# One chunk of 64 tokens handled as a tile of 128 rows and columns, and token norms in overlapping tiles of 128

## The chip, the core and the metric

The kernel runs on one core of a Trainium2 chip. The metric is the device time of one execution in microseconds. Before the change it is 2760.29 us, the median of three runs (2759.63 to 2760.55). The engines are named as in the profile: PE multiplies matrices (PEld loads its stationary operand), DVE, ACT and POOL work elementwise, SP and POOL issue DMAs.

## What is computed

One layer is applied to 2048 prompt tokens and to 64 sample tokens, which have a state of their own. Its parts, cut to what matters:

```python
h = rms_norm(x, g_pre)
vA, bA, cA, zA, q, f, iv, zB, gA, gB = split_cols(h @ w_in)      # ten products of 1024 columns
yA = (silu(zA) * bA * causal_conv3(cA * vA)) @ w_a_out           # path A
fg = lb + (1 - lb) * sigmoid(f); logf = log(fg); k = 1 - fg      # path B, 8 heads of 128
for each chunk of 64 tokens:                                     # hgrn2_block, S is 128 x 128 a head
    b = cumsum(logf); ref = b at the middle of the chunk
    att = tril((q * exp(b - ref)) @ (k * exp(ref - b)).T)
    o = att @ v + (q * exp(b)) @ S
    S = exp(b_last) * S + (k * exp(b_last - b)).T @ v
yB = (o * rsqrt(mean(o * o)) * g_onorm * silu(zB)) @ w_b_out
out = (sigmoid(gA) * yA + sigmoid(gB) * yB) @ w_o
x = x + rms_norm(out, g_post)
x = x + (p @ w_ple_proj) * sigmoid(rms_norm(x, g_ple) @ w_ple_gate)
```

All of it is float32. The outputs are both token streams, the last two inputs of the convolution and the states S.

## The kernel before

The 2112 tokens lie in one row: 1344 of the prompt, the 64 of the sample, the other 704 of the prompt. They are taken in three blocks of 704, features on partitions and tokens on columns, so that a block is done in two halves of 352 columns (`HN`). Each large product is made of seven smaller ones (`sgroup`, `in_turn`: Strassen-like sums of weight blocks), and each float32 product is taken as three passes over a high and a low part (lines 343 to 345, 436 to 438, 469 to 471). One such pass is a matmul record of `128x352`. Weights are streamed from memory by SP.

A block runs path B (eight heads), then path A, then the merging products, the output product, the norms and the gate. Path B is the part that the change touches:

- `head_prep` makes the operands of a head in two `sgroup`s: queries `qe`, keys `kb` (for the second chunk of a pair already scaled), the keys `ka` of the first chunk of each pair packed side by side (line 761), values `vt`, `qx` for the product with the state, and the gate `z`.
- `head_attn` does the attention of a head for one part of a block. A block has 11 chunks of 64: ten go in pairs of 128 tokens, and the last is alone. So there are three parts (`plan`): part 0 with four pairs, part 1 with one pair, part 2 with the single chunk at columns 640 to 704 (in block 1 that chunk is the sample). Three blocks, eight heads and three parts make 72 runs of `head_attn`, 24 of each part.
- `head_attn` has four steps, each cut by a `yield`. Step 0 transposes keys and values (799, 801), copies them to SBUF on ACT (803, 804), and multiplies keys by queries (813, 815); DVE puts the result under a causal mask into the part's own buffer `att` (817, 819). Step 1 multiplies keys by values (825) and forms the states on DVE (842, 846). Step 2 multiplies by `att` (862) and by the state before (864) and takes the norm of each row (868 to 871, `rstd_of` on DVE and POOL). Step 3 transposes back (876) and applies the gate (878).
- `path_b` puts these steps into a list of hooks, first step 0 of the three parts, then step 1, and so on, with `keep_z` as the fourteenth and last. After each of the seven products of an `sgroup` one hook runs. So the attention of a head is spread over the two `sgroup`s of the next head, and `placed()` ties its matmuls on PE behind the product that has just been issued: on PE they always stand between two stretches of `128x352` records.

With the pairs every matmul of step 1 to 3 has 128 rows and 128 columns of stationary operand. With the single chunk they have 64 of one or both, and in part 1 the product with `ka` has 64 columns (line 812).

The token norms of a half (`rms`, `col_rstd`, `spread`) sum over features with a matmul by ones, which puts tokens on partitions: 352 tokens are tiles of 128, 128 and 96. `rstd_of` scales on DVE and raises to the power -0.5 on POOL, once for the full tiles and once for the 96. A matmul with the identity spreads the result again. `row_rstd` does the same from token rows for the next block.

Tiles come from pools. A tag has a number of buffers, and a tile waits until a buffer of its tag has been read for the last time. Those that matter here: `one` (8 buffers, the small tiles of parts 1 and 2), `s0` (2), `state` (`NH + 2` = 10).

Of the kernel before, what the change touches and what calls it, by code (L numbers as in the profile page):

```python
# [18 lines left out]
P = 128  # L19
# [63 lines left out]
def hybrid_step(  # L83
# [39 lines left out]
    def hf(n=HN):  # L123
        return ring.tile([P, HN], F32, tag="hf", name=nm("hf"), bufs=HALVES)[:, :n]
# [32 lines left out]

    def constants():
        tri = rt(P)
        G.memset(tri, 1.0)  # L160
        G.affine_select(
            out=tri, in_=tri, pattern=[[1, P]], compare_op=ALU.is_ge, fill=0.0, base=0, channel_multiplier=-1
        )
        V.tensor_copy(caus, tri)
        V.memset(keep, 1.0)
        V.memset(keep.rearrange("p (c t) -> p c t", t=CH)[:, :, 0:1], 0.0)
        for t in atts:
            V.memset(t, 0.0)
# [354 lines left out]
    def tiles_of(n):  # L523
        return [(i, i * P, min(P, n - i * P)) for i in range((n + P - 1) // P)]

    def rstd_of(ms_ap, out_ap, scale):
        V.tensor_scalar(out_ap, ms_ap, scale, EPS, ALU.mult, ALU.add)
        shape = [out_ap.shape[0], out_ap.shape[1]]
        G.tensor_tensor(out_ap, out_ap, mhalf[: shape[0], :].to_broadcast(shape), ALU.pow)
# [21 lines left out]
    def col_rstd(acc, n):  # L551

        pc = ps_attn()
        cols = cols_tile(n)
        with placed():
            for i, o, ln in tiles_of(n):
                T.matmul(pc[:ln, i : i + 1], acc[:, o : o + ln], ones, start=True, stop=True)
        nf = n // P
        if nf:
            rstd_of(pc[:, :nf], cols[:, :nf], 1.0 / D)  # L560
        if n % P:
            rstd_of(pc[: n % P, nf : nf + 1], cols[: n % P, nf : nf + 1], 1.0 / D)
        return cols
# [23 lines left out]
    def row_rstd(bl, out):  # L587

        out.extend(cols_tile(HN) for _ in bl["segs"])
        todo = [(cols, s["t0"] + o, i, ln) for cols, s in zip(out, bl["segs"]) for i, o, ln in tiles_of(HN)]  # L590
        nxt = []
        for n in range(0, len(todo) + 2, 2):
            now, nxt = nxt, []
            for cols, o, i, ln in todo[n : n + 2]:
                xts = [rt(512), rt(512)]
                for q, xt in enumerate(xts):
                    G.dma_start(xt[:ln], x_tok[o : o + ln, q * 512 : q * 512 + 512])
                nxt.append((cols, i, ln, xts))
            for cols, i, ln, xts in now:
                sc = small.tile([P, 2], F32, tag="ss2", name=nm("ss2"))  # L600
                for q, xt in enumerate(xts):
                    A.activation(xt[:ln], xt[:ln], AF.Square, accum_out=sc[:ln, q : q + 1])
                V.tensor_tensor(sc[:ln, 0:1], sc[:ln, 0:1], sc[:ln, 1:2], ALU.add)
                rstd_of(sc[:ln, 0:1], cols[:ln, i : i + 1], 1.0 / D)
# [115 lines left out]
    def head_prep(bl, hc, hd, first):  # L720
# [21 lines left out]
        ka, kb, qx, vt, z = hf(), rt(), rt(), rt(), rt()  # L742

        def scaled(after):
# [36 lines left out]
    def head_attn(ip, gs, d, hd):  # L781

        nt, ln = len(gs), gs[0]["len"]
        o0, n = gs[0]["off"], nt * ln
        qe, z, att = d["qe"], d["z"], atts[ip]

        def tile3():
            if nt == 1:
                return small.tile([P, 1, P], F32, tag="one", name=nm("one"), bufs=8)
            return cols3(rt(nt * P), nt)  # L790

        def keys(g):
            return d["kb"][:, g["off"] : g["off"] + ln]
# [3 lines left out]
        with placed():  # L797
            for i, g in enumerate(gs):
                T.transpose(p_k[:ln, i * P : i * P + P], keys(g), ident)
            for i, g in enumerate(gs):  # L800
                T.transpose(p_v[:ln, i * P : i * P + P], d["vt"][:, g["off"] : g["off"] + ln], ident)
        kt, v = tile3(), tile3()
        A.copy(kt[:ln], cols3(p_k, nt)[:ln])
        A.copy(v[:ln], cols3(p_v, nt)[:ln])
        p_a = ps_attn()
        with placed():
            for i, g in enumerate(gs):
                o = g["off"]
                if nt > 1:
                    own, rows = d["ka"][:, o // 2 : o // 2 + P], P  # L810
                else:
                    own, rows = d["ka"][:, o // 2 : o // 2 + CH] if ln == P else keys(g), CH
                T.matmul(p_a[:rows, i * P : i * P + CH], own, qe[:, o : o + CH], start=True, stop=True)
# [9 lines left out]
        with placed():  # L823
            for i in range(nt):
                T.matmul(p_u[:, i * P : i * P + P], kt[:ln, i, :], v[:ln, i, :], start=True, stop=True)  # L825
# [3 lines left out]
        if sample:  # L829
            cur = small.tile([P, P], F32, tag="s0", name=nm("s0"), bufs=2)  # L830
# [13 lines left out]
        if g["end"]:  # L844
            end = small.tile([P, P], F32, tag="state", name=nm("state"), bufs=NH + 2)
# [12 lines left out]
        with placed():  # L858
            for i, g in enumerate(gs):
                o = g["off"]  # L860
                dst = p_o[:ln, i * P : i * P + P]
                T.matmul(dst, att[:ln, i, :ln], v[:ln, i, :], start=True, stop=prevs[i] is None)  # L862
                if prevs[i] is not None:
                    T.matmul(dst, d["qx"][:, o : o + ln], prevs[i], start=False, stop=True)  # L864
        on = tile3()
        ms = small.tile([P, 4], F32, tag="ms", name=nm("ms"))
        po3 = cols3(p_o, nt)
        A.activation(on[:ln], po3[:ln], AF.Square)
        V.tensor_reduce(ms[:ln, :nt], on[:ln], axis=mybir.AxisListType.X, op=ALU.add)
        rstd_of(ms[:ln, :nt], ms[:ln, :nt], 1.0 / P)  # L870
        V.tensor_tensor(on[:ln], po3[:ln], ms[:ln, :nt].unsqueeze(2).to_broadcast([ln, nt, P]), ALU.mult)
        yield
        p_t = ps_attn()
        with placed():
            for i in range(nt):
                T.transpose(p_t[:, i * ln : i * ln + ln], on[:ln, i, :], ident[:ln, :ln])
        c = slice(o0, o0 + n)
        V.scalar_tensor_tensor(z[:, c], p_t[:, :n], g_on[:, hd : hd + 1], z[:, c], ALU.mult, ALU.mult)
# [344 lines left out]
```

## Time and profile before

| | |
|---|---|
| median of the runs shown | 2760.29 us |
| time of the profiled execution | 2764.13 us |
| its span in the profile | 2761.8 us |
| mean granted clock of PE | 0.987 |
| ACT busy | 1449.9 us (52%) |
| POOL busy | 377.3 us (14%) |
| bytes moved | 748.37 MB, mean 271 GB/s |
| POOL `pow` of line 529, for `ms` and `cols` | 72 and 40 instructions |

The span is counted from the first to the last record of the profile; the execution's own time is 2.3 us longer. A line of the timeline has the start, the duration, the engine, the line of the kernel, the operation, output and input by the program's names, for a matmul its rows and columns of stationary operand (`64*128`), and the shape of the moving one (`64x128`). A float32 matmul is two records, a transpose one. Ends of matmuls are modelled and overlap the next one, so that the distance from one start to the next says what a matmul costs, not its duration.

### The profile page before, as it was taken

To read this page: it belongs to the slowest core of one execution; us is meant where nothing else is said; L and a number is where in the kernel's file an instruction comes from. 1 tells how busy PE (TensorE), PEld (TensorE's weight loads), DVE (VectorE), ACT (ScalarE), POOL (GpSimd) and SP (SyncE) were. 2 spreads that over 40 slices of the span, in tenths; PEclk is the share of its full clock that TensorE was granted. 3 is DMA by queue.
4 is the path that set the end of the run, shared out by engine and by line. 5 is a ranking of instruction groups with operands and counts; after the bars stand their busy time and mean duration, and the time that the engine had idled before them with its cause. 6 is when DMAs were issued, how large, how long until landed. Compare 5 with 4: busy or idle time off the path is not lost.

```text
span 2761.8 us, 47890 instructions
## 1 busy us (share of the span) xinstructions
PE 2683.5 (97%) x16736; PEld 2608.6 (94%) x16736; DVE 1718.2 (62%) x3338; ACT 1449.9 (52%) x2796; POOL 377.3 (14%) x698
## 2 busy tenths in 40 slices
PE   6999999999999999999999999999999999999998
PEld 5999999999999999999999999999999999999988
DVE  6788888899657544455645567453355554357764
ACT  4665565454324554566654555454555554445654
POOL 2000001110332211011111210021000000010022
PEclk7999999999999999999999999999999999999999
DMA  5767767888987898766689998599866668888878
GB/s 199 267 237 272 253 240 277 284 308 292 351 314 274 318 320 272 232 210 214 220 271 335 388 336 261 166 358 305 275 210 207 207 218 261 271 287 303 279 234 314
DMA packets 365553, 748.37 MB, mean 271 GB/s; under 512 B 44704, under 2 KB 48320, under 8 KB 365312
## 3 DMA queue, kind: packets, MB, share of 16 engines
q1 hardware_dynamic: 325728, 589.84, 64.3%
q0 software_dynamic: 39296, 155.44, 15.4%
q8 instruction: 132, 2.16, 0.3%
q14 instruction: 109, 0.89, 0.1%
q10 hardware_dynamic: 288, 0.05, 0.0%
HBM read 537.77 MB, written 207.37 MB: 270 GB/s over the span
## 4 chain that ended last, share of the span: by engine, by line
PE 78%; DMA 8%; issue 4%; DVE 4%; POOL 2%; ACT 1%; DVEq 0%; POOLq 0%; ACTq 0%; SPq 0%
PE pg L343 18%; PE pg L344 17%; PE pg L345 17%; PE pg L436 3%; PE pg L437 3%; PE pg L471 3%; PE pg L438 3%; PE pg L469 3%; PE pg L470 3%; DMA raw<-w_blk 2%; DMA raw<-S 1%; PE pa L825 1%; PE pa L862 1%; PE pa L864 1%; DMA r<-w_blk 1%
## 5 line engine op out<-in xcount | busy, mean ns | idle before, releaser
L343 PE MATMUL pg<-r,hi 128*128 128x352 f32 x3360 | 1116.7, 333 | 12.7 <-ACT r L182 5.9
L344 PE MATMUL pg<-r,hi 128*128 128x352 f32 x3360 | 1089.7, 325 | 4.9 <-DVE r L183 4.9
L213 ACT CAST hi<-raw 128x512 fp32r<-128x512 f32 x740 | 456.0, 619 | 633.2 <-PE pg L344 233.2
L345 PE MATMUL pg<-r,lo 128*128 128x352 f32 x2400 | 779.4, 325 | 5.2 <-DMA lo<-low 4.6
L343 PEld LDWEIGHTS pg<-r,hi 128*128 128x128 f32 x3360 | 633.8, 189 | 31.6 <-ACT hf L359 11.3
L344 PEld LDWEIGHTS pg<-r,hi 128*128 128x128 f32 x3360 | 635.4, 189 | 9.5 <-DVE r L183 9.5
L345 PEld LDWEIGHTS pg<-r,lo 128*128 128x128 f32 x2400 | 453.3, 189 | 7.3 <-DMA lo<-low 6.4
L345 PE MATMUL pg<-r,s 128*128 128x352 f32 x960 | 310.9, 324 | 0.6 <-DMA s<-low 0.6
L469 PE MATMUL pg<-r,hi 128*128 128x352 f32 x896 | 290.8, 326 | 2.7 <-ACT r L182 2.4
L470 PE MATMUL pg<-r,hi 128*128 128x352 f32 x896 | 291.6, 326 | 1.3 <-DVE r L183 1.0
L471 PE MATMUL pg<-r,lo 128*128 128x352 f32 x728 | 237.2, 326 | 7.6 <-DVE lo L183 6.2
L182 ACT CAST r<-r 128x352 fp32r<-128x352 f32 (+2 forms) x294 | 162.9, 589 | 143.1 <-DVE r L962 43.7
L182 ACT CAST hi<-raw 128x512 fp32r<-128x512 f32 (+1 forms) x232 | 138.0, 597 | 188.0 <-PE pg L344 51.7
L183 DVE TENSOR_TENSOR r<-r,r 128x352 fp32r<-128x352 f32 (+2 forms) x294 | 183.5, 649 | 61.9 <-ACT r L182 61.1
L183 DVE TENSOR_TENSOR lo<-raw,hi 128x512 fp32r<-128x512 f32 (+1 forms) x232 | 151.7, 657 | 76.6 <-ACT hi L182 66.3
L436 PE MATMUL pg<-r,hi 128*128 128x352 f32 x560 | 183.0, 331 | 9.3 <-ACT r L182 9.3
L437 PE MATMUL pg<-r,hi 128*128 128x352 f32 x560 | 183.9, 329 | 0.8 <-DVE r L183 0.6
L345 PEld LDWEIGHTS pg<-r,s 128*128 128x128 f32 x960 | 180.6, 188 | 1.0 <-DMA s<-low 0.9
L182 ACT CAST hi<-s 128x512 fp32r<-128x512 f32 x160 | 99.0, 619 | 151.8 <-PE pg L344 146.4
L469 PEld LDWEIGHTS pg<-r,hi 128*128 128x128 f32 x896 | 169.6, 190 | 5.0 <-ACT r L182 3.9
L470 PEld LDWEIGHTS pg<-r,hi 128*128 128x128 f32 x896 | 169.8, 190 | 2.8 <-DVE r L183 2.6
L359 ACT COPY hf<-pg 128x352 f32<-128x352 f32 x360 | 158.3, 446 | 0.5 <-PE pg L345 0.5
(317 smaller groups left out, 3985.1 us busy)
## 6 DMA issues: line engine op xcount, KB each, us to landing
raw<-w_blk SPq DMA_DIRECT2D x588, 256.0 KB, 4.0
lo<-low SPq DMA_DIRECT2D x422, 256.0 KB, 3.9
raw<-S SPq DMA_DIRECT2D x400, 256.0 KB, 4.1
low<-lo SPq DMA_DIRECT2D x344, 256.0 KB, 3.5
s<-low SPq DMA_DIRECT2D x318, 256.0 KB, 3.8
S<-s SPq DMA_DIRECT2D x160, 256.0 KB, 3.2
r<-x_fm POOLq DMA_DIRECT2D x40, 352.0 KB, 6.8
r<-w_blk POOLq DMA_DIRECT2D x48, 256.0 KB, 7.1
```

The source lines that it names most:

```text
L182: A.copy(hi, src)
L183: V.tensor_tensor(lo, src, hi.bitcast(F32), ALU.subtract)
L213: A.copy(hi, raw)
L343: add(hi[:, k, :], xhi, start=start and k == 0, stop=False)
L344: add(hi[:, k, :], xlo, start=False, stop=False)
L345: last[0] = add(lo[:, k, :], xhi, start=False, stop=k == KH - 1).ins
L359: copied = A.copy(got[n], ps[bank])
L436: add(hi[:, k, :], xhi, start=start and k == 0, stop=False)
L437: add(hi[:, k, :], xlo, start=False, stop=False)
L469: T.matmul(ps, hi[:, k % 4, :], xhi[:, c], start=k == 0, stop=False)
L470: T.matmul(ps, hi[:, k % 4, :], xlo[:, c], start=False, stop=False)
L471: last[0] = T.matmul(ps, lo[:, k % 4, :], xhi[:, c], start=False, stop=k == KB - 1).ins
```

## The change

The single chunk is read as the last 128 columns of the block, that is with the chunk before it in front. Its keys, values and output rows are put into three constant tiles (`lone`) of which the first half is zero and stays so; its part of `att` is the lower right quarter, and the rest of `att` is zero. So each matmul of the single chunk has 128 rows and columns. The first product of part 1 reads 128 columns of `ka`, for which `ka` becomes 384 wide and takes a sixth chunk. The norms over tokens take three tiles of 128 at 0, 128 and 224, which overlap by 32, and one `rstd_of` for all three. Besides, `one` has 5 buffers in place of 8, `s0` 1 in place of 2, `state` 9 in place of 10. In `row_rstd` (not shown) the same tiles are used, so that loads and operations of 96 rows become 128.

```diff
@@ -121,7 +121,7 @@
     def hf(n=HN):
-        return ring.tile([P, HN], F32, tag="hf", name=nm("hf"), bufs=HALVES)[:, :n]
+        return ring.tile([P, HN + 32], F32, tag="hf", name=nm("hf"), bufs=HALVES)[:, :n]
@@ -155,6 +155,8 @@
+    lone = [const.tile([P, 1, P], F32, tag=f"lone{i}", name=f"lone{i}") for i in range(3)]
@@ -164,7 +166,7 @@
         V.memset(keep.rearrange("p (c t) -> p c t", t=CH)[:, :, 0:1], 0.0)
-        for t in atts:
+        for t in atts + lone:
             V.memset(t, 0.0)
@@ -521,12 +523,13 @@
     def tiles_of(n):
-        return [(i, i * P, min(P, n - i * P)) for i in range((n + P - 1) // P)]
-    def rstd_of(ms_ap, out_ap, scale):
+        return [(i, min(i * P, n - P)) for i in range((n + P - 1) // P)]
+    def rstd_of(ms_ap, out_ap, scale, start=0):
         V.tensor_scalar(out_ap, ms_ap, scale, EPS, ALU.mult, ALU.add)
         shape = [out_ap.shape[0], out_ap.shape[1]]
-        G.tensor_tensor(out_ap, out_ap, mhalf[: shape[0], :].to_broadcast(shape), ALU.pow)
+        G.tensor_tensor(out_ap, out_ap, mhalf[start : start + shape[0], :].to_broadcast(shape), ALU.pow)
@@ -535,10 +538,8 @@
         with placed():
-            for i, o, ln in tiles_of(n):
-                T.matmul(
-                    pb[:, o : o + ln], cols[:ln, i : i + 1].to_broadcast([ln, P]), ident[:ln, :ln], start=True, stop=True
-                )
+            for i, o in tiles_of(n):
+                T.matmul(pb[:, o : o + P], cols[:, i : i + 1].to_broadcast([P, P]), ident, start=True, stop=True)
         return pb[:, :n]
@@ -553,13 +554,9 @@
         with placed():
-            for i, o, ln in tiles_of(n):
-                T.matmul(pc[:ln, i : i + 1], acc[:, o : o + ln], ones, start=True, stop=True)
-        nf = n // P
-        if nf:
-            rstd_of(pc[:, :nf], cols[:, :nf], 1.0 / D)
-        if n % P:
-            rstd_of(pc[: n % P, nf : nf + 1], cols[: n % P, nf : nf + 1], 1.0 / D)
+            for i, o in tiles_of(n):
+                T.matmul(pc[:, i : i + 1], acc[:, o : o + P], ones, start=True, stop=True)
+        rstd_of(pc[:, : cols.shape[1]], cols, 1.0 / D)
         return cols
@@ -739,7 +736,7 @@
         f, r = qc[:, 0, :nch], qc[:, 1, :nch]
-        ka, kb, qx, vt, z = hf(), rt(), rt(), rt(), rt()
+        ka, kb, qx, vt, z = hf(HN + 32), rt(), rt(), rt(), rt()
@@ -755,11 +752,11 @@
             f1, f2 = f[:, 0 : 2 * npair : 2], f[:, 1 : 2 * npair : 2]
-            ka3 = ka[:, : npair * CH].rearrange("p (g t) -> p g t", t=CH)
+            ka3 = ka[:, : (nch + 1) // 2 * CH].rearrange("p (g t) -> p g t", t=CH)
             kb1 = kb[:, :np1].rearrange("p (g c t) -> p g c t", c=2, t=CH)[:, :, 0, :]
             V.tensor_tensor(kb, sf, lg, ALU.mult)
-            V.tensor_copy(ka3, kb1)
-            V.tensor_tensor(kb1, ka3, f2.unsqueeze(2).to_broadcast([P, npair, CH]), ALU.mult)
+            V.tensor_copy(ka3, chunks(kb)[:, 0:nch:2, :])
+            V.tensor_tensor(kb1, ka3[:, :npair, :], f2.unsqueeze(2).to_broadcast([P, npair, CH]), ALU.mult)
             V.tensor_tensor(f2, f2, f1, ALU.mult)
@@ -780,54 +777,58 @@
-        def tile3():
+        single = ln < P
+        assert nt == 1 or not single
+        rows = slice(P - ln, P)
+        def tile3(i=None):
+            if single and i is not None:
+                return lone[i]
             if nt == 1:
-                return small.tile([P, 1, P], F32, tag="one", name=nm("one"), bufs=8)
+                return small.tile([P, 1, P], F32, tag="one", name=nm("one"), bufs=5)
             return cols3(rt(nt * P), nt)
-        def keys(g):
-            return d["kb"][:, g["off"] : g["off"] + ln]
+        def cols(t, g):
+            end = g["off"] + ln
+            return t[:, end - P : end]
...
             for i, g in enumerate(gs):
-                T.transpose(p_k[:ln, i * P : i * P + P], keys(g), ident)
+                T.transpose(p_k[:, i * P : i * P + P], cols(d["kb"], g), ident)
             for i, g in enumerate(gs):
-                T.transpose(p_v[:ln, i * P : i * P + P], d["vt"][:, g["off"] : g["off"] + ln], ident)
-        kt, v = tile3(), tile3()
-        A.copy(kt[:ln], cols3(p_k, nt)[:ln])
-        A.copy(v[:ln], cols3(p_v, nt)[:ln])
+                T.transpose(p_v[:, i * P : i * P + P], cols(d["vt"], g), ident)
+        kt, v = tile3(0), tile3(1)
+        A.copy(kt[rows], cols3(p_k, nt)[rows])
+        A.copy(v[rows], cols3(p_v, nt)[rows])
         p_a = ps_attn()
...
                 o = g["off"]
-                if nt > 1:
-                    own, rows = d["ka"][:, o // 2 : o // 2 + P], P
-                else:
-                    own, rows = d["ka"][:, o // 2 : o // 2 + CH] if ln == P else keys(g), CH
-                T.matmul(p_a[:rows, i * P : i * P + CH], own, qe[:, o : o + CH], start=True, stop=True)
-                if ln == P:
-                    T.matmul(p_a[:, i * P + CH : i * P + P], keys(g), qe[:, o + CH : o + P], start=True, stop=True)
+                if not single:
+                    T.matmul(p_a[:, i * P : i * P + CH], d["ka"][:, o // 2 : o // 2 + P], qe[:, o : o + CH], start=True, stop=True)
+                T.matmul(p_a[:, i * P + CH : i * P + P], cols(d["kb"], g), qe[:, o + ln - CH : o + ln], start=True, stop=True)
         pa3 = cols3(p_a, nt)
-        V.copy_predicated(att[:CH, :nt, :ln], caus[:CH, :ln].unsqueeze(1).to_broadcast([CH, nt, ln]), pa3[:CH, :, :ln])
-        if ln == P:
-            V.copy_predicated(att[CH:, :nt, CH:], caus[CH:, CH:].unsqueeze(1).to_broadcast([CH, nt, CH]), pa3[CH:, :, CH:])
+        if not single:
+            V.copy_predicated(att[:CH, :nt], caus[:CH].unsqueeze(1).to_broadcast([CH, nt, P]), pa3[:CH])
+        V.copy_predicated(att[CH:, :nt, CH:], caus[CH:, CH:].unsqueeze(1).to_broadcast([CH, nt, CH]), pa3[CH:, :, CH:])
         yield
...
             for i in range(nt):
-                T.matmul(p_u[:, i * P : i * P + P], kt[:ln, i, :], v[:ln, i, :], start=True, stop=True)
+                T.matmul(p_u[:, i * P : i * P + P], kt[:, i, :], v[:, i, :], start=True, stop=True)
         ss = tile3()
...
         if sample:
-            cur = small.tile([P, P], F32, tag="s0", name=nm("s0"), bufs=2)
+            cur = small.tile([P, P], F32, tag="s0", name=nm("s0"), bufs=1)
             G.dma_start(cur, s0[hd])
@@ -842,7 +843,7 @@
         if g["end"]:
-            end = small.tile([P, P], F32, tag="state", name=nm("state"), bufs=NH + 2)
+            end = small.tile([P, P], F32, tag="state", name=nm("state"), bufs=NH + 1)
             V.tensor_scalar(end, cur, d["eq"][:, c * CH + CH - 1 : c * CH + CH], None, ALU.mult)
@@ -857,25 +858,24 @@
             for i, g in enumerate(gs):
-                o = g["off"]
-                dst = p_o[:ln, i * P : i * P + P]
-                T.matmul(dst, att[:ln, i, :ln], v[:ln, i, :], start=True, stop=prevs[i] is None)
+                dst = p_o[:, i * P : i * P + P]
+                T.matmul(dst, att[:, i, :], v[:, i, :], start=True, stop=prevs[i] is None)
                 if prevs[i] is not None:
-                    T.matmul(dst, d["qx"][:, o : o + ln], prevs[i], start=False, stop=True)
-        on = tile3()
+                    T.matmul(dst, cols(d["qx"], g), prevs[i], start=False, stop=True)
+        on = tile3(2)
         ms = small.tile([P, 4], F32, tag="ms", name=nm("ms"))
         po3 = cols3(p_o, nt)
-        A.activation(on[:ln], po3[:ln], AF.Square)
-        V.tensor_reduce(ms[:ln, :nt], on[:ln], axis=mybir.AxisListType.X, op=ALU.add)
-        rstd_of(ms[:ln, :nt], ms[:ln, :nt], 1.0 / P)
-        V.tensor_tensor(on[:ln], po3[:ln], ms[:ln, :nt].unsqueeze(2).to_broadcast([ln, nt, P]), ALU.mult)
+        A.activation(on[rows], po3[rows], AF.Square)
+        V.tensor_reduce(ms[rows, :nt], on[rows], axis=mybir.AxisListType.X, op=ALU.add)
+        rstd_of(ms[rows, :nt], ms[rows, :nt], 1.0 / P, P - ln)
+        V.tensor_tensor(on[rows], po3[rows], ms[rows, :nt].unsqueeze(2).to_broadcast([ln, nt, P]), ALU.mult)
         yield
...
             for i in range(nt):
-                T.transpose(p_t[:, i * ln : i * ln + ln], on[:ln, i, :], ident[:ln, :ln])
+                T.transpose(p_t[:, i * P : i * P + P], on[:, i, :], ident)
         c = slice(o0, o0 + n)
-        V.scalar_tensor_tensor(z[:, c], p_t[:, :n], g_on[:, hd : hd + 1], z[:, c], ALU.mult, ALU.mult)
+        V.scalar_tensor_tensor(z[:, c], p_t[:, P - ln : P - ln + n], g_on[:, hd : hd + 1], z[:, c], ALU.mult, ALU.mult)
         yield
```

More of the change, by code (lines that the diff above doesn't have):

```diff
@@ L589, in row_rstd @@
         out.extend(cols_tile(HN) for _ in bl["segs"])
-        todo = [(cols, s["t0"] + o, i, ln) for cols, s in zip(out, bl["segs"]) for i, o, ln in tiles_of(HN)]
+        todo = [(cols, s["t0"] + o, i) for cols, s in zip(out, bl["segs"]) for i, o in tiles_of(HN)]
         nxt = []
@@ L593, in row_rstd @@
             now, nxt = nxt, []
-            for cols, o, i, ln in todo[n : n + 2]:
+            for cols, o, i in todo[n : n + 2]:
                 xts = [rt(512), rt(512)]
                 for q, xt in enumerate(xts):
-                    G.dma_start(xt[:ln], x_tok[o : o + ln, q * 512 : q * 512 + 512])
-                nxt.append((cols, i, ln, xts))
-            for cols, i, ln, xts in now:
+                    G.dma_start(xt, x_tok[o : o + P, q * 512 : q * 512 + 512])
+                nxt.append((cols, i, xts))
+            for cols, i, xts in now:
                 sc = small.tile([P, 2], F32, tag="ss2", name=nm("ss2"))
                 for q, xt in enumerate(xts):
-                    A.activation(xt[:ln], xt[:ln], AF.Square, accum_out=sc[:ln, q : q + 1])
-                V.tensor_tensor(sc[:ln, 0:1], sc[:ln, 0:1], sc[:ln, 1:2], ALU.add)
-                rstd_of(sc[:ln, 0:1], cols[:ln, i : i + 1], 1.0 / D)
+                    A.activation(xt, xt, AF.Square, accum_out=sc[:, q : q + 1])
+                V.tensor_tensor(sc[:, 0:1], sc[:, 0:1], sc[:, 1:2], ALU.add)
+                rstd_of(sc[:, 0:1], cols[:, i : i + 1], 1.0 / D)
             yield
```

## Prediction

> **What bounds the kernel.** I read the page first: busy times, then the chain of waits.
>
> ```profile
> span 2761.8 us, 47890 instructions
> PE 2683.5 (97%) x16736; PEld 2608.6 (94%) x16736; DVE 1718.2 (62%) x3338; ACT 1449.9 (52%) x2796; POOL 377.3 (14%) x698
> PE 78%; DMA 8%; issue 4%; DVE 4%; POOL 2%; ACT 1%; DVEq 0%; POOLq 0%; ACTq 0%; SPq 0%
> ```
>
> PE is the bound over the whole. As nearly all of the change lies in path B, I then read windows there: one head of block 0, and 40 us each of blocks 1 and 2 (columns: length, then busy time of PE, PEld, DVE, ACT, POOL with counts, granted clock, DMA share, GB/s).
>
> ```profile
> 213.10:263.90 50.80, 50.67 (x329) 48.58 (x328) 42.98 (x88) 28.73 (x54) 4.14 (x6) 1.00 0.72 255
> 1180.00:1220.00 40.00, 40.00 (x266) 38.16 (x265) 23.35 (x58) 24.07 (x44) 4.92 (x8) 1.00 0.69 217
> 2080.00:2120.00 40.00, 40.00 (x265) 37.86 (x264) 21.82 (x50) 23.15 (x46) 3.22 (x5) 1.00 0.66 209
> ```
>
> PE has no idle time there, at full clock, and DMA has a third or so to spare. Only DVE in block 0 comes near, with 85% of the head. So in path B a microsecond taken from PE is a microsecond of the span, and the question is what PE's small matmuls cost. Busy time doesn't tell it, as durations overlap; the distance of starts does. This is PE's timeline in the first head of block 0, cut to the last large record before a hook, the hook's records, and the second large record after it.
>
> ```profile
> 126.30 0.32 PE L345 MATMUL pg<-r,lo 128*128 128x352 f32 x1
> ...
> 126.78 0.33 PE L813 MATMUL pa<-r,hf 128*64 128x64 f32 x2
> ...
> 127.53 0.33 PE L344 MATMUL pg<-r,hi 128*128 128x352 f32 x1
> ...
> 129.15 0.32 PE L345 MATMUL pg<-r,lo 128*128 128x352 f32 x1
> ...
> 129.62 0.33 PE L813 MATMUL pa<-r,r 128*64 128x64 f32 x2
> ...
> 130.14 0.32 PE L344 MATMUL pg<-r,hi 128*128 128x352 f32 x1
> ...
> 131.74 0.33 PE L345 MATMUL pg<-r,lo 128*128 128x352 f32 x1
> 131.90 1.05 PE L825 MATMUL pa<-r,r 128*128 128x128 f32 x8
> ...
> 132.95 0.32 PE L344 MATMUL pg<-r,hi 128*128 128x352 f32 x1
> ...
> 136.71 0.32 PE L345 MATMUL pg<-r,lo 128*128 128x352 f32 x1
> 136.97 0.49 PE L825 MATMUL pa<-one,one 64*128 64x128 f32 x2
> ...
> 137.65 0.32 PE L344 MATMUL pg<-r,hi 128*128 128x352 f32 x1
> ...
> 145.14 0.32 PE L345 MATMUL pg<-r,lo 128*128 128x352 f32 x1
> 145.39 0.43 PE L862 MATMUL pa<-one,att 64*64 64x128 f32 x2
> 145.75 0.43 PE L864 MATMUL pa<-one,r 128*64 128x128 f32 x2
> ...
> 146.37 0.32 PE L344 MATMUL pg<-r,hi 128*128 128x352 f32 x1
> ...
> 152.27 0.32 PE L345 MATMUL pg<-r,lo 128*128 128x352 f32 x1
> 152.43 0.27 PE L876 MATMUL pa<-ident,one 128*128 128x128 f32 x1
> ...
> 152.70 0.33 PE L344 MATMUL pg<-r,hi 128*128 128x352 f32 x1
> ...
> 154.32 0.32 PE L345 MATMUL pg<-r,lo 128*128 128x352 f32 x1
> 154.57 0.27 PE L876 MATMUL pa<-ident,one 64*128 64x64 f32 x1
> ...
> 155.04 0.33 PE L344 MATMUL pg<-r,hi 128*128 128x352 f32 x1
> ```
>
> Large records follow each other every 0.16 us (131.74 to 131.90). What a hook costs PE is therefore the distance from its first to its last row above, less 0.32. A full-sized record costs little: the eight of line 825 take 132.95 - 131.74 - 0.32 = 0.89 us, 0.111 us each, and the full-sized transpose of part 1 takes 152.70 - 152.27 - 0.32 = 0.11 us. The odd shapes cost much more. The lone chunk's one product of line 825 takes 137.65 - 136.71 - 0.32 = 0.62 us for two records, its lone transpose 155.04 - 154.32 - 0.32 = 0.40 us for one. The reader is to see where it goes: after a large record at 136.71 the 64-row record starts 0.26 us later in place of 0.16, and PE goes on 0.68 us after that. PE pays on entering the odd shape and again on leaving it.
>
> **The terms on PE.** After the change each of these hooks is full-sized, so I price it at 0.111 us a record.
>
> - Part 1, step 0: 127.53 - 126.30 - 0.32 = 0.91 us now; then two transposes and two products of two records, 6 x 0.111 = 0.67. Gain 0.24.
> - Part 2, step 0: 130.14 - 129.15 - 0.32 = 0.67; then two transposes and one product, 4 x 0.111 = 0.44. Gain 0.23.
> - Part 2, step 1: 0.62; then 2 x 0.111 = 0.22. Gain 0.40.
> - Part 2, step 2: 146.37 - 145.14 - 0.32 = 0.91; then four records, 0.44. Gain 0.47.
> - Part 2, step 3: 0.40; then 0.11. Gain 0.29.
>
> That is 1.63 us for a head in a block. It recurs 24 times: a line's own view counts its records by shape (duration in ns, least, median, greatest; 48 are two for each of 24 products),
>
> ```profile
> L825 PE MATMUL pa<-one,one x96: 270/273/374, 134.7 to 2273.7; 128*128 128x128 f32 x48, 64*128 64x128 f32 x48
> ```
>
> and the timeline has, in the last head of block 2,
>
> ```profile
> 2273.25 0.33 PE L345 MATMUL pg<-r,s 128*128 128x352 f32 x1
> ...
> 2274.18 0.32 PE L344 MATMUL pg<-r,hi 128*128 128x352 f32 x1
> ```
>
> that is 2274.18 - 2273.25 - 0.32 = 0.61 us at step 1, to a hundredth as in the first. A wait for data that comes late would hardly be so regular. 24 x 1.63 = 39.1 us.
>
> Here a rule bears on the row. I count 11 changes of shape a head: two around part 1's narrow product, two around each of part 2's steps 0, 1 and 3, three in step 2 (64\*64, 128\*64, back). That is 1.63 / 11 = 0.148 us a change. The Trainium skill, TensorEngine Tiling (Array Packing), Key Properties, says that going from one tiling mode to another empties the array. TensorE: Matmul & The Clock Gate, Single matmul latency, puts an emptying at some 175 ns; by that the estimate would be 264 x 0.175 = 46 us and the time 2713. The rows are nearer to the kernel, and I keep 39.1.
>
> **Around it.** The wider products bring loads of 128 columns for 64, and the zero half costs no record more; if a wide load delayed PE, that is the second rival. DVE: the copy of line 761 goes from 320 to 384 columns, one mask copy is as large as before, three more memsets can run at the start, all under PE. ACT and POOL handle the same 64 rows, only higher up. The tiles `lone` are written in step 0 or 2 of a head and last read at most one step later, a head ahead of the next write; `one` gives five tiles a head in place of eight and has five. The load into `s0` now waits for the head before instead of two before. It is used a whole head later, so I cost it at nothing; if that cover were gone, it would be a DMA's landing a head in block 1 alone.
>
> **The norms.** For each half one scaling on DVE and one power on POOL go, 14 of the 40 powers, as line 529's own view counts them:
>
> ```profile
> L529 POOL TENSOR_TENSOR cols<-cols,mhalf x40: 527/697/1787, 30.3 to 2709.6; 96x1 f32<-96x1 f32 x18, 128x2 f32<-128x2 f32 x14, 128x1 f32<-128x1 f32 x8
> ```
>
> From the timeline of the start, and from the chain of waits at the end of block 0:
>
> ```profile
> 30.32 2.99 POOL L529 TENSOR_TENSOR cols<-cols,mhalf 128x2 f32<-128x2 f32 x4 [1.04 <-DVE cols L527]
> ...
> 34.59 1.81 DVE L613 SCALAR_TENSOR_TENSOR r<-r,vec,r 128x704 f32<-128x704 f32 x2
> ```
>
> ```profile
> 921.21 1.27 POOL cols L529 x2
> ```
>
> At the start everything waits for this chain: four powers in 2.99 us, the spreading, then line 613, which makes the first operands. Two powers at the shortest, 0.53 us, go: 1.1 us, between nothing (if the weights are later) and 1.5 (two at half of 2.99). Elsewhere the chain has such a pair, at 1.27 us, once at the end of block 0 and once of block 1, with PE fed beside it: nothing, at best 2 x 0.64. Against it the sums over 96 columns become 128 wide, at most 28 records by 0.06 us (192 less 132 ns, next fence), 1.7 us; as loads run beside PE's other work (PEld and PE are busy 94% and 97% at once), I take 0.3. Sum for the norms: -0.8 us, from -2.8 to +1.7.
>
> **Sum.** 39.1 + 0.8 = 39.9 us. The profiled execution took 2764.13 us, its span and 2.3 us around it; it becomes 2724.2. The runs shown have a median 3.8 us below the profiled one, which I leave as it is: 2760.29 - 39.9 = 2720.4 us.
>
> **Rivals.**
>
> *Wide loads cost.* The loads show it:
>
> ```profile
> L799 PEld LDWEIGHTS pa<-ident,r x144: 108/140/143, 121.7 to 2265.7; 128*128 128x128 f32 x120, 128*64 128x64 f32 x24
> L813 PEld LDWEIGHTS pa<-r,hf x240: 132/192/193, 122.6 to 2263.4; 128*128 128x128 f32 x96, 128*64 128x64 f32 x24
> ```
>
> Two transposes get 32 ns more and eight loads of products (two in part 1; two of 813, two of 862, two of 864 in part 2) 60 ns: 0.54 us a head, 13.0 us in all, and 2733.4 us. Against it: the full-sized records that set my 0.111 us have such loads already. Beside it stands the skill's page TensorE: Matmul & The Clock Gate, LDWEIGHTS, by which a load takes time by its columns and not by its rows; the rows above agree, 132 to 192 ns.
>
> *DVE holds block 0.* A head there shrinks from 50.80 to 49.2 us with 43.0 us of DVE work, 88%. If PE then waits for split weights, block 0's third, 8 x 1.63 = 13.0 us, is lost: 2733.4. For it: DVE also adds up weight blocks there; against it: 6 us a head are still free.
>
> *It isn't the shape.* If the gaps come from part 2 being a hook with one group, and not from 64 rows or columns, nothing is gained: 2760. Against it speaks part 1, a hook with one group too, whose transpose costs 0.11 us.
>
> *DVE stuck on a state, slower.* In block 1 each head makes two states, and with eight kept there were ten buffers; now there are nine. The sample's state (line 846) comes after the pair's, in step 1, and must wait until the head's old state has been read in step 2 by part 0's product.
>
> ```profile
> 1133.03 0.29 DVE L846 TENSOR_SCALAR state<-one,r 128x128 f32<-128x128 f32 x1
> 1134.76 0.52 DVE L383 TENSOR_TENSOR hf<-hf,pg 128x352 f32<-128x352 f32 x1 [1.45 <-PE pg L345]
> 1137.18 0.69 DVE L869 TENSOR_REDUCE ms<-r 128x4 f32<-128x512 f32 x1 [1.90 <-ACT r L868]
> ```
>
> Line 869 at 1137.18 already uses that product's result, so the wait ends within 4.2 us. Behind it stands line 383, which frees a PSUM bank of the large products. There are five banks, a product takes 12 x 0.16 = 1.9 us, and two can start before the bank is missed, so I cost the wait at nothing. Its full price on PE would be 8 x 4.2 = 33 us, still faster. It becomes slower only from 39.9 / 8 = 5.0 us a head: if the slot comes free only with part 2's step 2, which in the head above is 146.37 - 137.65 = 8.7 us after step 1, the price is 70 us and the time 2790.
>
> **How the numbers follow.** Forecast 0.82, its own range 2713 to 2727: the norms' bounds, a hundredth of a microsecond of reading on each of five terms and 24 heads (1.2 us), and two places at which another order at the seams of the blocks can win or cost 2 us. Wide loads 0.05, DVE in block 0 0.04, not the shape 0.04, slower 0.05. The range for eight in ten is 2711 to 2734, which takes in the two rivals that cost a third of the gain. Faster than before by over 0.2%, about what can be told from no change, is 0.91; within it 0.04; slower 0.05.
>
> **What would show it.** Right: no record with 64 rows or columns on PE; step 1 of part 2 at 0.22 us and step 3 at 0.11 between its large neighbours; a head of block 0 at 49.2 us; in windows of path B PE still without idle time. Wide loads: these hooks stand above 0.111 us a record. DVE in block 0: idle time of PE before lines 343 to 345, released by DVE. State: a wait of DVE at line 846 for line 864, and PE idle behind it in block 1 alone. The prediction is wrong if the hooks shrink and the span doesn't, or if they don't shrink.

## Result and profile after

The changed kernel takes 2729.49 us (median of 4 runs, 2726.84 to 2731.28) beside 2760.42 us: a ratio of 0.9883, 95% interval 0.9866 to 0.9900, 30.9 us less. A second set of runs gave 0.9894 (0.9880 to 0.9908). The forecast was 39.9 us less, 2720.4 us. The time lies in the range for eight in ten, 2711 to 2734, and outside the forecast's own, 2713 to 2727; three quarters of the gain came.

The page of the changed kernel, then windows of the same three kinds of stretch as before (length, busy time of PE, PEld, DVE, ACT, POOL, clock, DMA share, GB/s):

```profile
span 2726.6 us, 47857 instructions
PE 2646.6 (97%) x16736; PEld 2610.7 (96%) x16736; DVE 1721.8 (63%) x3327; ACT 1457.9 (53%) x2796; POOL 367.9 (13%) x684
```

```profile
208.48:258.58 50.10, 49.36 (x328) 48.55 (x327) 43.38 (x87) 29.14 (x54) 3.87 (x6) 1.00 0.74 259
1180.00:1215.50 35.50, 35.50 (x246) 35.38 (x245) 21.42 (x51) 22.12 (x42) 3.85 (x6) 1.00 0.70 219
2080.00:2115.50 35.50, 35.50 (x246) 35.38 (x245) 21.24 (x49) 22.14 (x43) 3.27 (x5) 1.00 0.72 224
```

PE is busy all the time in blocks 1 and 2, as before. In block 0, where it used to lack 0.13 us a head, it now lacks 0.74.

PE's timeline in the first head of block 0, the single chunk's steps 1, 2 and 3 between large records (lines have moved: 826 was 825, 345 to 347 were 343 to 345):

```profile
135.71 0.32 PE L347 MATMUL pg<-r,lo 128*128 128x352 f32 x1
135.87 0.38 PE L826 MATMUL pa<-lone,lone 128*128 128x128 f32 x2
...
136.25 0.33 PE L346 MATMUL pg<-r,hi 128*128 128x352 f32 x1
...
143.72 0.32 PE L347 MATMUL pg<-r,lo 128*128 128x352 f32 x1
143.88 0.38 PE L862 MATMUL pa<-lone,att 128*128 128x128 f32 x2
144.10 0.39 PE L864 MATMUL pa<-one,r 128*128 128x128 f32 x2
...
144.49 0.32 PE L346 MATMUL pg<-r,hi 128*128 128x352 f32 x1
...
152.48 0.32 PE L347 MATMUL pg<-r,lo 128*128 128x352 f32 x1
152.64 0.27 PE L876 MATMUL pa<-ident,lone 128*128 128x128 f32 x1
...
152.91 0.32 PE L346 MATMUL pg<-r,hi 128*128 128x352 f32 x1
```

Read as in the prediction, they cost 136.25 - 135.71 - 0.32 = 0.22 us (forecast 0.22, before 0.62), 0.45 (0.44, 0.91) and 0.11 (0.11, 0.40). Step 0, read in the same way from the same head, costs 126.74 - 125.75 - 0.32 = 0.67 us in part 1 (0.67, 0.91) and 129.13 - 128.35 - 0.32 = 0.46 in part 2 (0.44, 0.67). PE's terms came as priced. So the question is where eight microseconds of them went.

A head's length answers it. Its mark is the start of step 3 of part 0. Before, in block 0 and in block 1:

```profile
200.87 0.60 PE L876 MATMUL pa<-ident,r 128*128 128x128 f32 x4
...
251.63 0.60 PE L876 MATMUL pa<-ident,r 128*128 128x128 f32 x4
...
1182.54 0.60 PE L876 MATMUL pa<-ident,r 128*128 128x128 f32 x4
...
1219.60 0.60 PE L876 MATMUL pa<-ident,r 128*128 128x128 f32 x4
```

After:

```profile
198.25 0.60 PE L876 MATMUL pa<-ident,r 128*128 128x128 f32 x4
...
248.33 0.60 PE L876 MATMUL pa<-ident,r 128*128 128x128 f32 x4
...
1172.94 0.60 PE L876 MATMUL pa<-ident,r 128*128 128x128 f32 x4
...
1208.48 0.60 PE L876 MATMUL pa<-ident,r 128*128 128x128 f32 x4
```

Over the first six such distances of blocks 0 and 1 and all seven of block 2 the mean is 50.81 us before and 50.09 after in block 0, 37.10 and 35.54 in block 1, 37.13 and 35.50 in block 2. That is 0.72, 1.56 and 1.63 us a head, and 8 x (0.72 + 1.56 + 1.63) = 31.3 us, as much as the medians show. Block 0 gave less than half of the 1.63 us. The wait that took the rest stands in PE's timeline, in the products behind the second `sgroup` of the head. Before, one product has it:

```profile
213.27 0.32 PE L345 MATMUL pg<-r,lo 128*128 128x352 f32 x1
213.72 0.40 PE L343 MATMUL pg<-r,hi 128*128 128x352 f32 x1
213.96 0.33 PE L344 MATMUL pg<-r,hi 128*128 128x352 f32 x1
```

After, at two products in place of one:

```profile
208.48 0.32 PE L347 MATMUL pg<-r,lo 128*128 128x352 f32 x1
209.16 0.43 PE L345 MATMUL pg<-r,hi 128*128 128x352 f32 x1 [0.37 <-DVE r L770]
209.43 0.32 PE L346 MATMUL pg<-r,hi 128*128 128x352 f32 x1
...
211.06 0.32 PE L347 MATMUL pg<-r,lo 128*128 128x352 f32 x1
211.75 0.40 PE L345 MATMUL pg<-r,hi 128*128 128x352 f32 x1 [0.37 <-DVE r L392]
211.98 0.32 PE L346 MATMUL pg<-r,hi 128*128 128x352 f32 x1
```

Less the normal 0.32 us that is 0.37 us before and 0.63 + 0.60 = 1.23 us after; over the six heads the means are 0.42 and 1.27 us. Without these waits a head is 50.39 and 48.82 us long, 1.57 us apart: nearly the whole 1.63. Two lines on DVE end them. Line 770 (773 before) is the gate's product, which empties a PSUM bank, and line 392 (390 before) is a sum that empties another; PE has no bank for its next product until they have run. After the change PE waits for both, before it only for line 390. DVE's timeline shows how they come to be late. Before, from part 0's row norm (step 2) to these lines:

```profile
192.63 0.69 DVE L869 TENSOR_REDUCE ms<-r 128x4 f32<-128x512 f32 x1 [0.24 <-ACT r L868]
...
210.58 0.50 DVE L773 TENSOR_TENSOR r<-pg,r 128x352 f32<-128x352 f32 x1
...
213.08 0.50 DVE L390 TENSOR_TENSOR r<-hf,pg 128x352 f32<-128x352 f32 x1
```

After:

```profile
190.44 0.69 DVE L869 TENSOR_REDUCE ms<-r 128x4 f32<-128x512 f32 x1 [0.24 <-ACT r L868]
...
208.59 0.52 DVE L770 TENSOR_TENSOR r<-pg,r 128x352 f32<-128x352 f32 x1
...
211.09 0.51 DVE L392 TENSOR_TENSOR r<-hf,pg 128x352 f32<-128x352 f32 x1
```

For 18.0 us before and 18.2 after DVE works through a queue up to the gate's product, 20.45 and 20.65 up to the second line. Its longest pause is 1.2 us, for POOL's power in the row norm. The run begins when part 0's step 2 has left PE. PE's savings ahead of that point, 0.24 + 0.23 + 0.40 = 0.87 us, bring the whole run forward; less the 0.20 us by which the run has grown (why was not tried) that is 0.67, near the 0.72 that came. The savings behind it, part 2's steps 2 and 3 (0.47 + 0.29 = 0.76 us), only bring PE sooner to the end of a run that they don't shorten. This account is theory A; the experiments test it.

### The profile page after: what moved, and what is told of

Same layout as the page of the kernel before. It is cut to its first block, busy times and chain, and to the rows that moved or that the text cites. A ratio compares the mean times of both kernels' runs of the same rounds, so it can differ in the third digit from the quotient of the medians.

```text
span 2726.6 us, 47857 instructions
## 1 busy us (share of the span) xinstructions
PE 2646.6 (97%) x16736; PEld 2610.7 (96%) x16736; DVE 1721.8 (63%) x3327; ACT 1457.9 (53%) x2796; POOL 367.9 (13%) x684
## 4 chain that ended last, share of the span: by engine, by line
PE 78%; DMA 8%; DVE 4%; issue 4%; ACT 2%; POOL 1%; SPq 0%; DVEq 0%; POOLq 0%; ACTq 0%
PE pg L345 17%; PE pg L346 17%; PE pg L347 17%; PE pg L472 3%; PE pg L473 3%; PE pg L471 3%; PE pg L438 3%; PE pg L439 3%; PE pg L440 3%; DMA raw<-w_blk 2%; DMA raw<-S 1%; PE pa L826 1%; PE pa L862 1%; PE pa L864 1%; PE pa L816 1%
```

## Experiments

The rivals are B, the norms in wide tiles lost it; C, PE's waits in block 0 come from the order of the hooks or from the weights, and DVE is only the last of several; D, all hooks count in block 0 alike, and something else takes 0.9 us a head. "Before" beside each is the kernel before on the same chip. Lengths of heads are means over a block, as above, and those of blocks 1 and 2 agree to 0.05 us unless both are given.

**The norms alone.** The kernel before with the change's `tiles_of`, `rstd_of`, `spread`, `col_rstd` and `row_rstd`:

> The kernel before with the norms alone in overlapping tiles of 128; attention as before. Theory A (the hooks on PE give 39 us, and DVE in block 0 takes some 7 us back): the norms are worth 0 to 3 us, so 2757 to 2760 us. Rival B (the part of the gain that is missing was lost by the norms, whose narrow tiles became wide): 5 to 9 us slower than before, 2765 to 2769 us.

2763.78 us beside 2762.46, a ratio of 1.0003 (0.9993 to 1.0013), with heads of 50.81, 37.10 and 37.13 us, as in the kernel before.

**All but the norms.** The changed kernel with these five as before:

> The changed kernel with the norms as before (tiles of 128, 128 and 96, two powers a half); attention as changed. Theory A: 0 to 3 us above the changed kernel, 2729 to 2733 us, a head of block 0 at 50.1 us as there. Rival B: 5 to 9 us below it, 2720 to 2724 us.

2731.89 beside 2762.46, a ratio of 0.9894 (0.9880 to 0.9907), heads of 50.09 and 35.5 us. B falls: what the norms gave or took can't be told from zero (the interval above is -1.9 to +3.6 us), and block 0's heads are the same without them.

**The product for qx on POOL.**

```diff
-            V.tensor_tensor(chunks(qx), chunks(qe), f.unsqueeze(2).to_broadcast([P, nch, CH]), ALU.mult)
+            G.tensor_tensor(chunks(qx), chunks(qe), f.unsqueeze(2).to_broadcast([P, nch, CH]), ALU.mult)
```

> The changed kernel with the product that makes qx (line 762, 0.89 us on DVE a head) on POOL. It stands on DVE ahead of line 770, for which PE waits in block 0. Theory A: DVE reaches line 770 up to 0.9 us sooner, PE's two waits of a head in block 0 (0.7 us each between rows in place of 0.16) go for the most part, a head of block 0 falls from 50.1 to 49.2 to 49.5 us, the whole to 2722 to 2726 us. Rival C (the waits come from the order of the hooks or from the weights, and DVE is only the last of several): block 0 stays at 50.1 us and the time within 2 us of the changed kernel.

2740.45 beside 2762.46, 0.9923 (0.9910 to 0.9935): slower than the changed kernel, and its heads are 50.14 us in block 0, as C has it. But DVE wasn't relieved. These are DVE and POOL at the same time in this kernel's block 0:

```profile
204.08 1.59 DVE L185 TENSOR_TENSOR lo<-s,hi 128x512 fp32r<-128x512 f32 x1
```

```profile
203.75 1.37 POOL L762 TENSOR_TENSOR r<-r,qc 128x704 f32<-128x704 f32 x1 [4.90 <-DVE qc L760]
```

A split of weights that takes 0.69 us elsewhere took 1.59 us beside POOL's product, so what left DVE's queue came back as 0.90 us of delay. The run did not test what it was made for. The Trainium skill, SBUF — State Buffer, section SBUF: two separate sides, states this: an operation of DVE with two inputs from SBUF and one of GpSimd that reads SBUF exclude each other for a whole instruction. The two rows agree with it. The loss against the changed kernel lies elsewhere: the last head of block 0 and of block 1 grew from 52.14 to 56.86 us and from 37.62 to 41.98 us, where `row_rstd`'s loads share POOL's queue. These two heads vary without that product as well (block 1's was 36.41 us in a second profile of the changed kernel and 41.21 with the norms alone), so the queue is a place to look at, not a shown cause.

**The same in the kernel before.**

> The kernel before with the same product (its line 765) on POOL. Theory A: DVE was no bound before, but for 0.37 us a head in block 0, so at most 3 us are to be had, 2757 to 2760 us. If DVE's load as such costs time, it is faster by as much as in the changed kernel, 5 us or more.

2768.54 beside 2762.46, 1.0025 (1.0016 to 1.0034): slower too, with heads of 50.82 us on average and the same growth at the ends of blocks 0 and 1 (52.53 to 56.20, 38.71 to 43.03). The mean hides two kinds of head. In four, the split beside POOL's product takes 1.64 us, DVE's run to the gate's product is 18.1 to 18.2 us, PE waits 0.54 to 0.60 us and the head has 50.94 to 51.00; in two the run is 17.7, PE's wait is gone and the head has 50.49 and 50.52. So where DVE was relieved, PE's wait went, as A has it.

**The product for qx later, still on DVE.** This takes it from ahead of line 770 without a second engine.

```diff
-            V.tensor_tensor(chunks(qx), chunks(qe), f.unsqueeze(2).to_broadcast([P, nch, CH]), ALU.mult)
...
         sgroup(ZB * 8 + hd, IV * 8 + hd, hc, sink_v, first, mid=scaled)
+        V.tensor_tensor(chunks(qx), chunks(qe), f.unsqueeze(2).to_broadcast([P, nch, CH]), ALU.mult)
```

> The changed kernel with the product for qx (0.89 us on DVE a head) moved in the program behind the second sgroup of the head, still on DVE, so that it no longer stands ahead of line 770. Theory A (DVE's queue behind the third product of that sgroup holds PE in block 0): a head of block 0 falls from 50.1 us to between 49.2 and 49.5, those of blocks 1 and 2 stay at 35.5, the whole is 5 to 7 us below the changed kernel, 2722 to 2726 us. Rival C (the waits come from elsewhere): 50.1 us again, and the time of the changed kernel within 2 us.

2727.03 beside 2761.85, 0.9874 (0.9860 to 0.9887). Heads are 49.34 us in block 0 and 35.5 in the others, as A has it. PE's wait in this kernel:

```profile
207.93 0.32 PE L347 MATMUL pg<-r,lo 128*128 128x352 f32 x1
208.50 0.40 PE L345 MATMUL pg<-r,hi 128*128 128x352 f32 x1 [0.25 <-DVE r L769]
208.74 0.32 PE L346 MATMUL pg<-r,hi 128*128 128x352 f32 x1
```

One wait of 0.49 us is left, and 49.34 - 0.49 = 48.85 us is the length without it, the same as in the changed kernel. The run up to the gate's product is 17.91 us, only 0.24 shorter, since a tenth preparation of weights (lines 185 and 281) has moved into it; up to line 392 it is 19.81 in place of 20.65, and the wait behind that line is gone. C falls. This is the fastest of all that were run. Its lead over the changed kernel shows in block 0's heads (8 x 0.75 = 6.0 us); in the whole it is not shown, as the intervals overlap.

**The same move in the kernel before.**

> The same move in the kernel before. Theory A: only the 0.37 us a head that PE waited there can be won, so a head of block 0 goes from 50.8 to 50.4 to 50.5 us and the time by 2 to 3 us, 2757 to 2760 us. Rival: as much as in the changed kernel, 5 us or more, which would say that DVE was a bound of block 0 all along.

2761.17 beside 2761.85, 0.9996 (0.9987 to 1.0005), heads of 50.41 in block 0, as expected: DVE's run held PE before the change too, by 0.4 us. What that is worth in the whole, 3 us, does not show in the medians.

**The product for qx twice.**

```diff
             V.tensor_tensor(chunks(qx), chunks(qe), f.unsqueeze(2).to_broadcast([P, nch, CH]), ALU.mult)
+            V.tensor_tensor(chunks(qx), chunks(qe), f.unsqueeze(2).to_broadcast([P, nch, CH]), ALU.mult)
```

> The changed kernel with the product for qx done twice on DVE (the second writes the same values), 0.89 us more of DVE a head in front of line 770. Theory A: a head of block 0 goes up by nearly that, from 50.1 to about 51.0 us, those of blocks 1 and 2 stay at 35.5, the whole is up by 6 to 8 us, 2735 to 2738 us. Rival C: no head changes by more than 0.1 us.

2750.54 beside 2761.85, 0.9956 (0.9943 to 0.9968). Blocks 1 and 2 stay at 35.5 as A says, but block 0 goes to 53.20, three times what was expected. PE's timeline at one wait, then windows of this wait, of the stretch behind it and of the stretch behind the next head's wait:

```profile
211.06 0.32 PE L347 MATMUL pg<-r,lo 128*128 128x352 f32 x1
214.47 0.40 PE L345 MATMUL pg<-r,hi 128*128 128x352 f32 x1 [3.09 <-DVE r L771]
```

```profile
211.06:214.47 3.41, 0.32 (x4) 0.07 (x2) 3.41 (x7) 0.62 (x1) 0.00 (x0) 1.00 0.43 159
214.50:218.70 4.20, 4.20 (x18) 4.20 (x19) 3.30 (x8) 1.55 (x4) 0.60 (x1) 0.63 0.81 254
268.00:272.00 4.00, 3.82 (x24) 3.85 (x25) 3.55 (x10) 1.75 (x5) 0.60 (x1) 1.00 0.83 250
```

Two things were missing from the expectation. DVE's run to the gate's product is 20.7 us here, 2.6 more: 0.89 us for the second product, and the rest because twelve weight preparations (lines 185 and 281, 0.6 us each) stand in it and not nine, counted in the trace. DVE's instructions come in the same order in both profiles of the changed kernel, and an edit of the queue moves these by whole places. And PE's clock fell: the wait is 3.4 us in all six heads, behind four the granted clock was 0.62 to 0.65, and these heads have 53.65 to 53.79 us; behind two it stayed at 1.00, and they have 52.16 and 52.20. These two are 2.1 us longer than in the changed kernel: the 2.6 us of DVE's run, less the second wait of 0.6, which is gone.

**Step 1 of the single chunk over 64 rows again.**

```diff
-                T.matmul(p_u[:, i * P : i * P + P], kt[:, i, :], v[:, i, :], start=True, stop=True)
+                T.matmul(p_u[:, i * P : i * P + P], kt[rows, i, :], v[rows, i, :], start=True, stop=True)
```

> The changed kernel with step 1 of the single chunk taken over its 64 rows again (the product of line 826 over the upper half of the tiles), all else full-sized. The shape theory: that hook goes back from 0.22 to 0.62 us in all 24 heads, and a head of blocks 1 and 2 from 35.5 to 35.9 us. With theory A the same 0.40 us is hidden in block 0, where PE waits for DVE later in the same sgroups: 50.1 us again, and the whole is up by 16 x 0.40 = 6.4 us. If block 0's waits are not DVE's, its heads go to 50.5 too, and the whole is up by 9.6 us. If the shape costs nothing, nothing changes.

2741.59 beside 2761.85, 0.9929 (0.9916 to 0.9943). Heads: 35.93 and 35.89, up by 0.39 as the shape says. But 50.49 in block 0, up by 0.40, with PE's waits at 1.25 us for 1.27: the expectation drawn from A in its first form was wrong. The reason is in the run above: step 1 comes before part 0's step 2, where DVE's run begins, so a longer step 1 delays the run as well. That gave A its sharper form, which the next two tested.

**Step 3 of the single chunk over 64 rows and columns again.**

```diff
-                T.transpose(p_t[:, i * P : i * P + P], on[:, i, :], ident)
+                T.transpose(p_t[:, i * P + P - ln : i * P + P], on[rows, i, :], ident[rows, rows])
```

> The changed kernel with step 3 of the single chunk (its transpose, line 876) over 64 rows and columns again. Theory A in its sharper form: in block 0 PE waits at the end of a run of DVE work of some 18 us that begins with part 0's step 2; what PE saves behind that beginning, part 2's steps 2 and 3, only lengthens the wait. So heads of blocks 1 and 2 go up by 0.29 us to 35.8, a head of block 0 stays at 50.1, the whole is up by 16 x 0.29 = 4.6 us. Rival D (every hook counts in block 0, and its missing 0.9 us a head is one loss of another kind): block 0 goes to 50.4, the whole up by 7.0 us.

2738.00 beside 2761.54, 0.9916 (0.9902 to 0.9929). Heads: 50.08 in block 0, 35.80 and 35.82 in the others. What PE loses behind the beginning of DVE's run costs nothing in block 0 and all of it elsewhere. It comes off the wait: PE's two waits are 0.98 us a head here, 1.27 in the changed kernel. D falls.

**Step 2 of the single chunk over 64 rows and columns again.** Lines 862 and 864 with `att[rows, i, rows]`, `v[rows, i, :]`, 64 columns of `qx`, into `p_o[rows, ...]`.

> The changed kernel with step 2 of the single chunk (lines 862 and 864) over 64 rows and columns again. Theory A, sharper form: heads of blocks 1 and 2 up by 0.47 us to 36.0, a head of block 0 within 0.1 of 50.1, the whole up by 16 x 0.47 = 7.5 us. Rival D: block 0 to 50.55, the whole up by 11.3 us.

2754.86 beside 2761.54, 0.9973 (0.9962 to 0.9985). Heads: 36.02 and 35.99 as expected, but 52.12 in block 0, as neither theory had it. DVE's timeline of this kernel, from part 0's row norm to line 770, and windows behind PE's wait in this head and in the next:

```profile
194.04 0.69 DVE L869 TENSOR_REDUCE ms<-r 128x4 f32<-128x512 f32 x1 [0.24 <-ACT r L868]
...
213.60 0.68 DVE L185 TENSOR_TENSOR lo<-raw,hi 128x512 fp32r<-128x512 f32 x1
214.20 0.52 DVE L770 TENSOR_TENSOR r<-pg,r 128x352 f32<-128x352 f32 x1
```

```profile
214.90:219.00 4.10, 4.10 (x26) 4.10 (x27) 3.65 (x9) 2.08 (x6) 0.60 (x1) 1.00 0.82 286
266.50:271.00 4.50, 4.50 (x18) 4.50 (x19) 3.42 (x9) 1.80 (x5) 0.60 (x1) 0.63 0.91 276
```

The run is 20.16 us long, 2.0 more than the changed kernel's. Again twelve weight preparations stand in it in place of nine; one of them is the row just before line 770. That the mean of the heads is 2.03 us longer too is chance: four have 51.56 to 51.64 us, and two have 53.12 and 53.15, behind whose waits the granted clock was 0.62 and 0.63. What step 2's shape alone is worth can be read beside the run before with twelve preparations, qx twice, from the heads at full clock. There the run, head and wait are 20.75, 52.18 and 3.30 us, here 20.17, 51.60 and 2.34. Run and head are both shorter by 0.58, the wait by 0.96. So most of step 2's 0.47 us came off the wait here as well, as A has it.

**Both kernels once more.**

> The changed kernel unchanged, once more beside the others. If the difference between its heads (35 us less in the spans) and the medians (31 us) is the scatter of the stretches between the blocks, its heads are 50.1 and 35.5 us again to 0.05, and only those stretches differ, by 1 to 3 us each.

> The kernel before unchanged, for a second profile: heads of 50.8, 37.1 and 37.1 us to 0.05, the stretches between the blocks 1 to 3 us from those of the first profile.

The changed kernel: 2734.55 beside 2761.54, heads of 50.10, 35.54 and 35.49. The kernel before, one run: 2757.52, heads of 50.81, 37.10 and 37.13. From one profile of the kernel before to the other the span went from 2761.8 to 2755.1 us, all of it between the blocks and at the ends: 638.0 to 635.7 us from block 0's last head to block 1's first, 620.2 to 617.2 from block 1 to block 2. Path B's heads are the same to 0.05 us, but for the last one of block 0 (52.53 and 54.23). That is why the spans of the first two profiles differ by 35.2 us, the second two by 29.6, and the heads by 31.3.

## Why the prediction was right, and where it failed

*PE bound, hooks priced by the distance of starts.* Right to two hundredths of a microsecond for each, and whole in blocks 1 and 2: 1.56 and 1.63 us a head for 1.63. That it is the shape is shown by the three runs that take one step back: 0.39, 0.29 and 0.49 us a head there, where the terms were 0.40, 0.29 and 0.47.

*The emptied array.* The estimate of 46 us from the 175 ns of the Trainium skill (TensorE: Matmul & The Clock Gate, Single matmul latency) was too much. The 0.148 us a change from the rows were right: 1.56 and 1.63 us over 11 changes are 0.142 and 0.148. That an emptying of the array is what costs this time is argued; the runs show the price of the shape.

*"So in path B a microsecond taken from PE is a microsecond of the span."* This is the step that failed, for block 0. It gave 0.72 of 1.63 us a head, 7.3 us less in all. The rival that named DVE in block 0 had the place and the engine. It had PE waiting for split weights; the runs show PE waiting for banks that lines 770 and 392 empty, with the splits ahead of them in DVE's queue. It priced the loss at 13.0 us, where 7.3 came, and was given 0.04. The forecast's own range has no room for this loss; the time lies in the wider one because that reached down to the rivals' 2733.4 us. The error was one of reading: 85% of DVE is an average over a head of 51 us, which hides a run of 18 us, over nine tenths busy, that ends in what PE waits for. The row that showed it was in the profile before: 0.45 us between two large records at 213.27, in a block that the prediction read as without idle time of PE. The rival was waved off with 6 us of free time a head, but most of that time lies outside the run, in which DVE's pauses sum to 1.8 us. (43.0 of 49.2 us is 87%, not 88.)

*Norms, -0.8 us (from -2.8 to +1.7).* Nothing measurable, which the range allows. At the start the two powers did go, as costed, but that the path there is theirs was a misreading. POOL and DVE of the changed kernel:

```profile
29.90 1.89 POOL L532 TENSOR_TENSOR cols<-cols,mhalf 128x3 f32<-128x3 f32 x2 [1.09 <-DVE cols L530]
```

```profile
33.62 0.69 DVE L281 TENSOR_TENSOR s<-raw,raw 128x512 f32<-128x512 f32 x1
34.23 1.81 DVE L610 SCALAR_TENSOR_TENSOR r<-r,vec,r 128x704 f32<-128x704 f32 x2
```

The powers take 1.89 us for 2.99, and the first operands start at 34.23 for 34.59. But DVE goes over to them straight from a sum of weights, which itself starts 0.36 us sooner (33.62 for 33.98 at line 279 before). So the queue on DVE sets this start in both kernels, and none of the 0.36 us is shown to come from the powers. It is the case "if the weights are later", priced at nothing.

*Wide loads.* No cost: the hooks stand at 0.111 us a record.

*DVE stuck on a state.* It didn't happen. DVE of the changed kernel in block 1:

```profile
1127.20 0.52 DVE L385 TENSOR_TENSOR hf<-hf,pg 128x352 f32<-128x352 f32 x1 [1.38 <-PE pg L347]
1127.65 0.29 DVE L847 TENSOR_SCALAR state<-one,r 128x128 f32<-128x128 f32 x1
```

With nine buffers the sample's state (847) stands behind line 385, which it used to precede, and nothing waits for it.

## What to carry to other kernels

Price small matmuls by the distance of the large ones around them, in a full shape and in the odd one: what a 64-row piece saves in work it can lose several times over when its shape differs from its neighbours'. Before a saving on the busiest engine is counted in full, look in each stage for even its smallest idle gaps and what released them. If that is a run of another engine that starts from a fixed point of the first one's work, only what is saved ahead of that point counts; and that run's length can jump when an edit moves others' work into it. Read single stretches before explaining a mean: one that agrees with a theory can be made of two kinds that don't.

## What the runs showed of the hardware

PE's clock fell behind some waits, and the length of the wait alone does not decide it. From the start of one matmul to the next it was 3.4 us in all six heads of block 0 with qx twice: behind four the granted clock was 0.62 to 0.65 over some 4 us, behind two 1.00. With step 2 narrow it was 2.4 us in all six: behind two the clock was 0.62 and 0.63, behind four 1.00. A drop cost the head 1.5 us. With qx twice the clock's record has the four drops start at 160.99, 215.61, 321.42 and 427.23 us and last 3.41 us each, at half speed; they lie 16, 31 and 31 times 3.41 us apart. So it may be the place of a wait on such a grid that decides; that was not tried. The Trainium skill, TensorE: Matmul & The Clock Gate, Why this matters for your kernels, warns of gaps above about 3 us; as a bound these runs don't agree with it, as 2.4 us were enough twice.

And DVE's copy for `ka` became faster when it grew: 0.48 us for 128x320 (line 761 before), 0.35 for 128x384 (line 758), medians of 24 each. Why was not tried.
